# Second output projection of a two-block layer: second half of the outputs tile by tile, with the norm per tile

## The chip, the cores and the metric

One core of a Trainium2 chip runs the whole program. The metric is the device time of one execution in microseconds. Engines are named as the profile names them: PE (matmuls), PEld (weight loads of PE), DVE, ACT, POOL and SP; SP issues most transfers.

## What is computed

The program is two transformer blocks in a row on 512 tokens of width 1024. The change lies in the second block, between its mixer and its feed-forward part (names of the reference, shortened):

```python
merged = sigmoid(g_attn) * (attn @ w_attn_out) + sigmoid(g_hy) * (hy @ w_hy_out)
out = merged @ w_out                      # 512 x 1024 by 1024 x 1024
x = x + g1 * out
h = rmsnorm(x, norm_ffn_g) * (1 + sc2) + sh2
x = x + g2 * peer(h, wq, keys1, keys2, u_tab, v_tab)
```

`peer` looks up 16 of 16,384 experts per token and head. The kernel takes the rows of `u_tab` and `v_tab` for the last 128 tokens by gathers, and for the first 384 tokens multiplies by the whole tables.

## The kernel before

Tokens lie in four tiles of 128 (`NT` = 4, `ND` = 3 of them dense in `peer`). The tile framework takes the program as it is written, sets the order of each engine's instructions with its own timing model, and inserts the waits; each engine then runs its instructions in that order. A buffer of a pool (`bufs=n`) is taken over by the next tile of that name when the last reader of the old one is done.

Every fp32 product is made of three: `split` (L66 to L70) copies an operand to a rounded `hi` on ACT (L69) and subtracts it on DVE, or on POOL, to get `lo` (L70); `mm3` (L85 to L89) multiplies hi by hi, lo by hi and hi by lo. `wload` (L72) fetches a weight chunk of 512 KB into `wraw` (4 buffers) and splits it into `whi` and `wlo` (3 buffers each).

The stage in question is at the start of `peer`:

- `out_proj` (L431) multiplies `merged` (split as `mh`, `ml`) by `w2o`, which is 8 chunks: 4 for the first 512 outputs, 4 for the others. For each half it takes one PSUM bank (`bank`, 6 of them) per token tile, goes through the 4 chunks, and for each chunk through the tiles, 6 matmuls each (24 per tile and half). Then it adds the gated result to the residual `x` in two DVE operations (L452, L453).
- It is called twice, for tiles 0 to 2 and for tile 3 (`groups`, L1446), so the 8 chunks are fetched and split twice.
- Then the norm: `sumsq` (L859) squares a tile's row on ACT with a running sum (L863), `row_rstd` (L108 to L119) makes the inverse root in two DVE steps, one ACT root (L114) and four DVE steps, once for tiles 0 to 2 and once for tile 3. `modulated_tile` (L842) scales the row into `xn` (L847), transposes it on PE in 8 pieces of 128 x 128 (L853), evacuates each from PSUM with scale and shift into `hf` on DVE (L854), and splits that into `hph` and `hpl`, in two halves of 4 pieces.
- After the last tile is written down, `ahead(4)` (L1436) computes 4 of the 128 products of the dense part early: `u_chunk` (L1422) fetches and splits a chunk of `puT` (lo on POOL here), makes 24 matmuls on the first 384 tokens into `acc` (2 banks), applies gelu on ACT (L1430) and stores the result.
- `scores` (L1522) follows: the query projection (`pwq`) on all 512 tokens, the router's first product.

Of the kernel before, what the change touches and what calls it, by code (L numbers as in the profile page):

```python
# [9 lines left out]
F32 = mybir.dt.float32  # L10
F32R = mybir.dt.float32r
# [4 lines left out]
AF = mybir.ActivationFunctionType  # L16
ALU = mybir.AluOpType
# [4 lines left out]
D = 1024  # L22
KD = D // 128
NT = S // 128
# [22 lines left out]
class Emit:  # L47
# [383 lines left out]
    def out_proj(self, wd, mh, ml, tiles, gate=None, pool=None, fill=None):  # L431

        nc = self.nc
        for n in range(2):
# [11 lines left out]
            for p, t in zip(po, tiles):  # L446
# [3 lines left out]
                else:  # L450
                    tmp = pool.tile([128, 512], F32, name="gtmp", bufs=2)
                    nc.vector.tensor_tensor(tmp, p, gate[:, n * 512:(n + 1) * 512], op=ALU.mult)  # L452
                    nc.vector.tensor_tensor(xs, tmp, xs, op=ALU.add)  # L453


    def moe(self, fill):
        tc, nc, A = self.tc, self.nc, self.A
# [381 lines left out]
            self.split(hh[:, k, :128 * n], hl[:, k, :128 * n], f)  # L839
            yield xn  # L840

    def modulated_tile(self, t, rstd, a, b, hh, hl, pool):  # L842

        nc = self.nc
        xn = pool.tile([128, D], F32, name="xn", bufs=2)
        c = slice(t * 128, t * 128 + 128)
        nc.scalar.activation(xn, self.x[:, t], AF.Copy, scale=rstd)  # L847
        for kk in range(0, KD, 4):
            p = self.bank()
            f = pool.tile([128, 512], F32, name="hf", bufs=2)  # L850
            for k in range(4):
                o = slice(k * 128, k * 128 + 128)
                nc.tensor.transpose(p[:, o], xn[:, (kk + k) * 128:(kk + k) * 128 + 128], self.ident)  # L853
                nc.vector.tensor_scalar(f[:, o], p[:, o], a[:, kk + k:kk + k + 1], b[:, kk + k:kk + k + 1],  # L854
                                        op0=ALU.mult, op1=ALU.add)
            self.split(hh[:, kk:kk + 4, c], hl[:, kk:kk + 4, c], f.rearrange("p (k t) -> p k t", k=4))
        return xn

    def sumsq(self, pool, xs, n, name):  # L859
        ssq = self.small.tile([128, n], F32, name=name)  # L860
# [534 lines left out]
    def peer(self):  # L1395
        tc, nc, A = self.tc, self.nc, self.A
# [3 lines left out]
        ND = NT - 1  # L1400
# [4 lines left out]
        with ExitStack() as es:  # L1405
            pp = es.enter_context(tc.tile_pool(name="pp", bufs=1))
            hh = pp.tile([128, KD, S], F32R, name="hph")
            hl = pp.tile([128, KD, S], F32R, name="hpl")
# [11 lines left out]
            a = self.mod_cols(pp, self.mod, 4 * D, "pa", self.vec[:, V_GF2:V_GF2 + KD])  # L1420
            b = self.mod_cols(pp, self.mod, 3 * D, "pb")
            def u_chunk(c, eng=None):  # L1422

                wh, wl = self.wload(A["puT"][c], eng=eng)
                p = self.acc()
                for k in range(KD):
                    s_ = slice(k * 128, k * 128 + 128)
                    self.mm3(p[:, :TD], wh[:, s_], wl[:, s_], hh[:, k, :TD], hl[:, k, :TD], k == 0, k == KD - 1)
                g = dn.tile([128, TD], F32, name="ga", bufs=4)
                nc.scalar.activation(g, p[:, :TD], AF.Gelu_apprx_tanh)  # L1430
                if c < AHEAD:
                    self.dma(ad[c], g)
                    return None
                return g

            def ahead(n, eng=nc.gpsimd):  # L1436
                for _ in range(n):
                    if nu[0] < AHEAD:
                        u_chunk(nu[0], eng)
                        nu[0] += 1  # L1440

            nu = [0]
            with ExitStack() as e2s:
                pm = e2s.enter_context(tc.tile_pool(name="pm", bufs=1))
                mh, ml, g1, mg = self.merged
                groups = range(NT - 1), [NT - 1]  # L1446
                for tiles in groups:
                    self.out_proj(A["w2o"], mh, ml, tiles, gate=g1, pool=mg)
                for tiles in groups:
                    n = len(tiles)  # L1450
                    ssq = self.sumsq(pm, lambda j: self.x[:, tiles[j]], n, f"ssq{n}")
                    rstd = self.row_rstd(ssq, n, f"rr{n}")
                    for j, t in enumerate(tiles):
                        xn = self.modulated_tile(t, rstd[:, j:j + 1], a, b, hh, hl, pm)
                        if t == NT - 1:
                            ahead(4)
                r1 = pm.tile([128, D], F32, name="r1")
                r2 = pm.tile([128, D], F32, name="r2")
                self.dma(r1, self.mod[0:1, 4 * D:5 * D].to_broadcast([128, D]))
                self.dma(r2, A["g_ffn2"].to_broadcast([128, D]))  # L1460
                stt(r1, r1, 1.0, r2, op0=ALU.add, op1=ALU.mult)
                self.dma(r2, self.mod[0:1, 3 * D:4 * D].to_broadcast([128, D]))
                tt(ht, xn, r1, op=ALU.mult)
                tt(ht, ht, r2, op=ALU.add)

# [48 lines left out]
            with ExitStack() as ek:  # L1514
# [98 lines left out]
                for t in range(ND):  # L1613
                    c = slice(t * 32, t * 32 + 32)
                    p = self.bank()
# [13 lines left out]
            with ExitStack() as ek:  # L1629
# [8 lines left out]
                for t in range(ND):  # L1638
                    for q in range(32):

                        e = eT[:, t * 32 + q].rearrange("p j n i -> p (j n) i")
                        o = p2.tile([128, 8, 64, 2], F16, name="oh", bufs=3)
                        tt(o, ih[:, None].to_broadcast([128, 8, 64, 2]),
                           e[:, 0:8, None].to_broadcast([128, 8, 64, 2]), op=ALU.is_equal)
                        w = p2.tile([128, 8, 64, 2], F16, name="ohw", bufs=3)
# [3 lines left out]
                        p = self.bank()  # L1649
                        for i in range(4):  # L1650
                            for j in range(2):
# [3 lines left out]
                                             scale=1.0 / WSCALE)  # L1655
                        n = 32 * t + q + 1
# [290 lines left out]
```

## Time and profile before

| | us |
|---|---|
| median of 3 runs | 2715.93 |
| lowest and highest run | 2709.26 and 2721.87 |
| the profiled execution | 2710.84 |
| its span in the profile | 2709.1 |
| PE busy, share of the span | 2445.6 (90%) |
| DVE busy | 1824.4 (67%) |
| ACT busy | 1090.5 (40%) |
| POOL busy | 939.3 (35%) |

The span is the time from the first to the last instruction that the profile shows; the 1.7 us between it and the profiled execution lie around it. Busy shares are averages over stages with different limits. PEclk is the clock that was granted to PE: 1.00 is 2.4 GHz, 0.50 is 1.2 GHz. In a timeline the brackets hold an engine's idle time before an instruction and what ended it.

### The profile page before, as it was taken

The page shows a single profiled execution, that of the slowest core. Times are in us where ns is not written, and L with a number is a line of the kernel's source. Part 1 is how long each engine was busy: PE and PEld are TensorE (multiplying, and loading weights), DVE is VectorE, ACT ScalarE, POOL GpSimd, SP SyncE. Part 2 cuts the span into 40 slices and gives each one's busy share as a digit, 9 for nine tenths or more (in the row PEclk, how much of TensorE's full clock was granted, in tenths as well). Part 3 has the DMA queues.
Part 4 walks back from the last instruction along what each step waited for, and adds up shares of the span by engine and source line. Part 5 has one row for each costly group of instructions (what it writes and reads, how often), then busy time and mean ns, then how long its engine had stood idle before and what let it go on. Part 6 is the DMA issues. An engine that isn't in the chain of part 4 may idle for free.

```text
span 2709.1 us, 33479 instructions
## 1 busy us (share of the span) xinstructions
PE 2445.6 (90%) x11725; PEld 1911.1 (71%) x11725; DVE 1824.4 (67%) x3149; ACT 1090.5 (40%) x1688; POOL 939.3 (35%) x777
## 2 busy tenths in 40 slices
PE   7999897879977988989798889989899999999997
PEld 6776566423335766668587778979688878888886
DVE  6677965334346576564648889977877767767676
ACT  5555434212215336653444554434433333333233
POOL 1002640111100310000145665420676765666661
PEclk9999998889988988999899999989899999999998
DMA  4114684789975211104534448997699988888884
GB/s 143 63 56 170 226 291 159 283 336 391 400 274 212 94 59 47 39 31 144 186 114 136 148 159 305 348 347 276 197 299 301 305 299 266 291 300 284 275 294 152
DMA packets 215934, 589.47 MB, mean 218 GB/s; under 512 B 30565, under 2 KB 85349, under 8 KB 214740
## 3 DMA queue, kind: packets, MB, share of 16 engines
q1 hardware_dynamic: 170836, 433.91, 45.9%
q0 software_dynamic: 44928, 153.42, 16.1%
q8 instruction: 92, 1.51, 0.2%
q14 instruction: 78, 0.64, 0.1%
HBM read 541.85 MB, written 53.78 MB: 220 GB/s over the span
## 4 chain that ended last, share of the span: by engine, by line
PE 30%; DVE 12%; DMA 10%; issue 9%; ACT 4%; POOL 3%; POOLq 0%; SPq 0%; DVEq 0%; ACTq 0%
DMA wraw<-puT 5%; PE acc L87 4%; PE acc L89 4%; PE acc L88 4%; PE yp L87 4%; PE yp L88 4%; PE yp L89 4%; DMA grow<-pvr,ei 3%; POOL grow L1493 2%; DVE wlo L70 2%; DMA gd<-gs 1%; PE bank L87 1%; PE bank L89 1%; PE bank L88 1%; DVE gy L1510 1%
## 5 line engine op out<-in xcount | busy, mean ns | idle before, releaser
L69 ACT ACTIVATE whi<-wraw 128x1024 fp32r<-128x1024 f32 (+1 forms) x290 | 300.0, 1035 | 478.1 <-PE acc L88 164.2
L87 PE MATMUL acc<-hph,whi 128*128 128x384 f32 (+1 forms) x1152 | 404.3, 351 | 20.8 <-ACT ga L1430 19.9
L89 PE MATMUL acc<-hph,wlo 128*128 128x384 f32 (+1 forms) x1152 | 402.6, 350 | 6.5 <-DVE wlo L70 5.6
L88 PE MATMUL acc<-hpl,whi 128*128 128x384 f32 (+1 forms) x1152 | 399.4, 347 | 0.0
L70 DVE TENSOR_TENSOR wlo<-wraw,whi 128x1024 fp32r<-128x1024 f32 (+1 forms) x242 | 294.9, 1220 | 138.4 <-ACT whi L69 136.5
L70 POOL TENSOR_TENSOR wlo<-wraw,whi 128x1024 fp32r<-128x1024 f32 x48 | 115.7, 2416 | 481.4 <-ACT whi L69 468.2
L87 PE MATMUL yp<-vhi,wah 128*128 128x512 f32 x732 | 231.0, 395 | 17.4 <-ACT wah L69 17.4
L87 PEld LDWEIGHTS acc<-hph,whi 128*128 128x128 f32 x1152 | 220.5, 191 | 32.8 <-ACT ga L1430 24.6
L89 PEld LDWEIGHTS acc<-hph,wlo 128*128 128x128 f32 x1152 | 220.2, 191 | 19.5 <-DVE wlo L70 12.1
L88 PE MATMUL yp<-vlo,wah 128*128 128x512 f32 x732 | 231.1, 395 | 0.0
L89 PE MATMUL yp<-vhi,wal 128*128 128x512 f32 x732 | 228.3, 395 | 0.0
L88 PEld LDWEIGHTS acc<-hpl,whi 128*128 128x128 f32 x1152 | 220.5, 191 | 7.1 <-DVE hpl L70 0.2
L1685 POOL TENSOR_TENSOR gw<-gw,ga 128x256 f32<-128x256 f32 x128 | 175.8, 1374 | 137.9 <-DMA ga<-ad 76.7
L1493 POOL DMA_INDIRECT grow<-pu,ei x128 | 151.0, 1179 | 209.4 <-DVE grow L1506 173.3
L70 DVE TENSOR_TENSOR vlo<-wraw,vhi 128x1024 fp32r<-128x1024 f32 x122 | 157.6, 1292 | 93.5 <-ACT vhi L69 93.5
L1493 POOL DMA_INDIRECT grow<-pvr,ei x128 | 177.0, 1383 | 119.4 <-DVE gy L1510 96.3
L69 ACT ACTIVATE wah<-gw 128x384 fp32r<-128x384 f32 x126 | 66.2, 526 | 276.7 <-POOL gw L1686 223.3
L1510 DVE SCALAR_TENSOR_TENSOR gy<-grow,wt,gy 128x1024 f32<-128x1024 f32 x127 | 164.0, 1291 | 16.2 <-DMA grow<-pvr,ei 14.2
L87 PEld LDWEIGHTS yp<-vhi,wah 128*128 128x128 f32 x732 | 139.8, 191 | 47.8 <-ACT wah L69 20.4
L70 DVE TENSOR_TENSOR wal<-gw,wah 128x384 fp32r<-128x384 f32 x126 | 94.1, 747 | 104.2 <-ACT wah L69 103.7
L89 PEld LDWEIGHTS yp<-vhi,wal 128*128 128x128 f32 x732 | 139.6, 191 | 31.1 <-DVE wal L70 1.8
L88 PEld LDWEIGHTS yp<-vlo,wah 128*128 128x128 f32 x732 | 139.6, 191 | 27.7
(671 smaller groups left out, 5154.6 us busy)
## 6 DMA issues: line engine op xcount, KB each, us to landing
wraw<-wgu SPq DMA_DIRECT2D x128, 512.0 KB
wraw<-puT SPq DMA_DIRECT2D x128, 512.0 KB
wraw<-pv SPq DMA_DIRECT2D x128, 512.0 KB
wraw<-wd SPq DMA_DIRECT2D x64, 512.0 KB
aw<-wada SPq DMA_DIRECT2D x48, 512.0 KB
gd<-gs SPq DMA_DIRECT2D x8, 2048.0 KB
gw<-gd SPq DMA_DIRECT2D x128, 128.0 KB
ad<-ga SPq DMA_DIRECT2D x80, 192.0 KB
```

What stands on the lines that cost most here:

```text
L69: nc.scalar.activation(hi, src, AF.Copy)
L70: (eng or nc.vector).tensor_tensor(lo, src, f32(hi), op=ALU.subtract)
L87: mm(ps, lhsT=wh, rhs=xh, start=first, stop=False)
L88: mm(ps, lhsT=wh, rhs=xl, start=False, stop=False)
L89: mm(ps, lhsT=wl, rhs=xh, start=False, stop=last)
L1493: nc.gpsimd.indirect_dma_start(out=r, out_offset=None, in_=A["pu" if i < 128 else "pvr"], in_offset=bass.IndirectOffsetOnAxis(ap=ei[:, s:s ...
L1510: stt(gy, r, wt[:, s:s + 1], gy, op0=ALU.mult, op1=ALU.add)
L1685: nc.gpsimd.tensor_tensor(gw[:, :TG], gw[:, :TG], g[:, :TG], op=ALU.mult)
```

## The change

- A new generator `out_proj_tiles` makes the first half of the outputs for all four tiles (4 banks, 4 chunks). It then fetches the 4 chunks of the other half once and keeps them: two in buffers of their own (`wo..`), two in the usual `whi` and `wlo`. The gated adds of the first half follow, and then each tile gets its 24 matmuls of the second half, its gated add, and is yielded.
- For each tile that is yielded, the caller makes the sum of squares (written into `xn` instead of a buffer of its own), `row_rstd` for this tile alone, and `modulated_tile`. In it the pieces are evacuated in turn by DVE and by ACT.
- `ahead(4, None)` is called behind tile 2 instead of behind tile 3, and its `lo` parts are subtracted on DVE.
- The loads of `r1` and `r2`, which `htok` needs, are written ahead of the stage.

```diff
@@ -451,6 +451,47 @@
                     tmp = pool.tile([128, 512], F32, name="gtmp", bufs=2)
                     nc.vector.tensor_tensor(tmp, p, gate[:, n * 512:(n + 1) * 512], op=ALU.mult)
                     nc.vector.tensor_tensor(xs, tmp, xs, op=ALU.add)
+
+    def out_proj_tiles(self, wd, mh, ml, gate, pool, wpool):
+
+
+        nc = self.nc
+
+        def add(p, t, n):
+            o = slice(n * 512, n * 512 + 512)
+            tmp = pool.tile([128, 512], F32, name="gtmp", bufs=2)
+            nc.vector.tensor_tensor(tmp, p, gate[:, o], op=ALU.mult)
+            nc.vector.tensor_tensor(self.x[:, t, o], tmp, self.x[:, t, o], op=ALU.add)
+
+        def mms(p, t, c, w):
+            for kk in range(2):
+                k, o = 2 * c + kk, slice(kk * 512, kk * 512 + 512)
+                self.mm3(p, mh[:, k, t * 128:(t + 1) * 128], ml[:, k, t * 128:(t + 1) * 128],
+                         w[0][:, o], w[1][:, o], k == 0, k == KD - 1)
+
+        ps = [self.bank() for _ in range(NT)]
+        for c in range(4):
+            w = self.wload(wd[c])
+            for t in range(NT):
+                mms(ps[t], t, c, w)
+        ws = []
+        for c in range(4):
+            if c < 2:
+                r = self.wraw.tile([128, 1024], F32, name="wraw")
+                self.dma(r, wd[4 + c])
+                w = [wpool.tile([128, 1024], F32R, name=f"wo{i}{c}", bufs=1) for i in range(2)]
+                self.split(w[0], w[1], r)
+            else:
+                w = self.wload(wd[4 + c])
+            ws.append(w)
+        for t in range(NT):
+            add(ps[t], t, 0)
+        for t in range(NT):
+            p = self.bank()
+            for c in range(4):
+                mms(p, t, c, ws[c])
+            add(p, t, 1)
+            yield t
 
 
     def moe(self, fill):
@@ -839,10 +880,9 @@
             self.split(hh[:, k, :128 * n], hl[:, k, :128 * n], f)
             yield xn
 
-    def modulated_tile(self, t, rstd, a, b, hh, hl, pool):
+    def modulated_tile(self, t, rstd, a, b, hh, hl, pool, xn):
 
         nc = self.nc
-        xn = pool.tile([128, D], F32, name="xn", bufs=2)
         c = slice(t * 128, t * 128 + 128)
         nc.scalar.activation(xn, self.x[:, t], AF.Copy, scale=rstd)
         for kk in range(0, KD, 4):
@@ -851,10 +891,13 @@
             for k in range(4):
                 o = slice(k * 128, k * 128 + 128)
                 nc.tensor.transpose(p[:, o], xn[:, (kk + k) * 128:(kk + k) * 128 + 128], self.ident)
-                nc.vector.tensor_scalar(f[:, o], p[:, o], a[:, kk + k:kk + k + 1], b[:, kk + k:kk + k + 1],
-                                        op0=ALU.mult, op1=ALU.add)
+                if k % 2:
+                    nc.scalar.activation(f[:, o], p[:, o], AF.Identity, scale=a[:, kk + k:kk + k + 1],
+                                         bias=b[:, kk + k:kk + k + 1])
+                else:
+                    nc.vector.tensor_scalar(f[:, o], p[:, o], a[:, kk + k:kk + k + 1], b[:, kk + k:kk + k + 1],
+                                            op0=ALU.mult, op1=ALU.add)
             self.split(hh[:, kk:kk + 4, c], hl[:, kk:kk + 4, c], f.rearrange("p (k t) -> p k t", k=4))
-        return xn
 
     def sumsq(self, pool, xs, n, name):
         ssq = self.small.tile([128, n], F32, name=name)
@@ -1443,23 +1486,20 @@
             with ExitStack() as e2s:
                 pm = e2s.enter_context(tc.tile_pool(name="pm", bufs=1))
                 mh, ml, g1, mg = self.merged
-                groups = range(NT - 1), [NT - 1]
-                for tiles in groups:
-                    self.out_proj(A["w2o"], mh, ml, tiles, gate=g1, pool=mg)
-                for tiles in groups:
-                    n = len(tiles)
-                    ssq = self.sumsq(pm, lambda j: self.x[:, tiles[j]], n, f"ssq{n}")
-                    rstd = self.row_rstd(ssq, n, f"rr{n}")
-                    for j, t in enumerate(tiles):
-                        xn = self.modulated_tile(t, rstd[:, j:j + 1], a, b, hh, hl, pm)
-                        if t == NT - 1:
-                            ahead(4)
                 r1 = pm.tile([128, D], F32, name="r1")
                 r2 = pm.tile([128, D], F32, name="r2")
                 self.dma(r1, self.mod[0:1, 4 * D:5 * D].to_broadcast([128, D]))
                 self.dma(r2, A["g_ffn2"].to_broadcast([128, D]))
                 stt(r1, r1, 1.0, r2, op0=ALU.add, op1=ALU.mult)
                 self.dma(r2, self.mod[0:1, 3 * D:4 * D].to_broadcast([128, D]))
+                for t in self.out_proj_tiles(A["w2o"], mh, ml, g1, mg, pm):
+                    xn = pm.tile([128, D], F32, name="xn", bufs=2)
+                    ssq = self.small.tile([128, 1], F32, name="ssq1")
+                    nc.scalar.activation(xn, self.x[:, t], AF.Square, accum_out=ssq)
+                    rstd = self.row_rstd(ssq, 1, "rr1")
+                    self.modulated_tile(t, rstd, a, b, hh, hl, pm, xn)
+                    if t == ND - 1:
+                        ahead(4, None)
                 tt(ht, xn, r1, op=ALU.mult)
                 tt(ht, ht, r2, op=ALU.add)
```

What it moves on PE, at the end of the projection. Before, the last matmuls of the projection (`bank_9302` is tile 3's second half) stand ahead of all transposes (`xn_9371` is tile 0's, `xn_9397` tile 1's); further on the u products (`acc_9494`) follow tile 2's last transposes:

```order
L89 MATMUL bank_9302<-whi_9341,ml2_8546 128x512
L853 MATMUL bank_9373<-ident_73,xn_9371 128x128 [waits Activation_49]
L853 MATMUL bank_9385<-ident_73,xn_9371 128x128
L853 MATMUL bank_9373<-ident_73,xn_9371 128x128 [waits DVE_49]
L853 MATMUL bank_9399<-ident_73,xn_9397 128x128 [waits Activation_49]
...
L853 MATMUL bank_9437<-ident_73,xn_9423 128x128 [waits DVE_49]
L87 MATMUL acc_9494<-hph_9010,whi_9490 128x384 [waits Activation_49]
L87 MATMUL acc_9528<-hph_9010,whi_9524 128x384
L88 MATMUL acc_9494<-hpl_9011,whi_9490 128x384 [waits DVE_49]
```

With the change (`bank_9200` is the second half of tile 0, `bank_9266` of tile 1, `bank_9332` of tile 2; `xn_9228` is tile 0's row, `xn_9294` tile 1's):

```order
L89 MATMUL bank_9200<-whi_9184,ml2_8546 128x512
L893 MATMUL bank_9242<-ident_73,xn_9228 128x128 [waits Activation_49]
L893 MATMUL bank_9254<-ident_73,xn_9228 128x128 [waits DVE_49]
L87 MATMUL bank_9266<-wo00_9166,mh2_8545 128x512 [waits DVE_49]
L88 MATMUL bank_9266<-wo10_9167,mh2_8545 128x512
...
L893 MATMUL bank_9242<-ident_73,xn_9228 128x128 [waits Activation_49]
L893 MATMUL bank_9254<-ident_73,xn_9228 128x128 [waits Activation_49]
L893 MATMUL bank_9242<-ident_73,xn_9228 128x128 [waits DVE_49]
L893 MATMUL bank_9254<-ident_73,xn_9228 128x128 [waits DVE_49]
L893 MATMUL bank_9308<-ident_73,xn_9294 128x128 [waits Activation_49]
L893 MATMUL bank_9320<-ident_73,xn_9294 128x128
L87 MATMUL bank_9332<-wo00_9166,mh2_8545 128x512
```

The 24 matmuls of tile 0 are now followed by two transposes of tile 0, which wait for ACT, and then by the matmuls of tile 1; the other transposes of tile 0 stand among and behind these, and two of tile 1 ahead of tile 2's matmuls.

On DVE, from the add of tile 1 on (`gtmp_9291` is tile 1's; `hf_9243` and `hf_9255` hold tile 0's transposed halves; `rr1v_9297` begins tile 1's row factor), the rest of tile 0 and the norm of tile 1 now stand in each other's places:

```order
L898 TENSOR_SCALAR hf_9255<-bank_9254,pa_9026,pb_9029 128x128 [waits PE_49]
L463 TENSOR_TENSOR gtmp_9291<-bank_9266,g1_8547 128x512 [waits PE_49]
L898 TENSOR_SCALAR hf_9243<-bank_9242,pa_9026,pb_9029 128x128 [waits PE_49]
L898 TENSOR_SCALAR hf_9255<-bank_9254,pa_9026,pb_9029 128x128 [waits PE_49]
L464 TENSOR_TENSOR x_tok_8534<-gtmp_9291,x_tok_8534 128x512 [waits DVE_49]
L70 TENSOR_TENSOR hpl_9011<-hf_9243,hph_9010 128x4x128 [waits DVE_49,Activation_49]
L112 TENSOR_SCALAR rr1v_9297<-ssq1_9295 128x1 [waits Activation_49]
L113 RECIPROCAL rr1l_9299<-rr1v_9297 128x1 [waits DVE_49]
L70 TENSOR_TENSOR hpl_9011<-hf_9255,hph_9010 128x4x128 [waits Activation_49]
```

The evacuations of tile 0's third pieces come ahead of the add of tile 1, and a split of tile 0 ahead of and inside tile 1's row factor.

On PE ahead of the router (`acc_9596` and `acc_9506` are the fourth u product before and now, `acc_9665` and `acc_9635` the router's first). Before:

```order
L88 MATMUL acc_9596<-hpl_9011,whi_9592 128x384
L89 MATMUL acc_9596<-hph_9010,wlo_9593 128x384
L87 MATMUL acc_9665<-hph_9010,whi_9661 128x512 [waits Activation_49]
L88 MATMUL acc_9665<-hpl_9011,whi_9661 128x512 [waits DVE_49]
L89 MATMUL acc_9665<-hph_9010,wlo_9662 128x512 [waits Pool_49]
```

With the change:

```order
L89 MATMUL acc_9506<-hph_9010,wlo_9503 128x384
L893 MATMUL bank_9576<-ident_73,xn_9562 128x128 [waits Activation_49]
L893 MATMUL bank_9588<-ident_73,xn_9562 128x128 [waits Activation_49]
L893 MATMUL bank_9576<-ident_73,xn_9562 128x128 [waits DVE_49]
L893 MATMUL bank_9588<-ident_73,xn_9562 128x128 [waits DVE_49]
L87 MATMUL acc_9635<-hph_9010,whi_9631 128x512 [waits Activation_49]
```

The last transposes, tile 3's, have moved from inside the u products to right ahead of the router's first matmul.

## Rows read from the trace of the kernel before

**Rows 1.** Windows over the stage: busy us of each engine, then PEclk.

```profile
core 0: us, PE busy (x) PEld busy (x) DVE busy (x) ACT busy (x) POOL busy (x), PEclk, DMA share, GB/s
1283.99:1330.62 46.63, 46.10 (x192) 35.68 (x192) 27.82 (x34) 19.06 (x23) 0.70 (x1) 1.00 0.58 188
1330.62:1355.41 24.79, 9.72 (x27) 4.50 (x27) 18.98 (x43) 10.97 (x17) 7.14 (x4) 0.59 0.49 176
1355.41:1358.86 3.45, 3.45 (x11) 3.23 (x11) 1.91 (x4) 0.47 (x1) 0.00 (x0) 0.50 0.00 0
1358.86:1374.82 15.96, 15.96 (x93) 15.50 (x93) 3.57 (x8) 6.72 (x9) 3.93 (x4) 1.00 0.26 78
1380.00:1420.00 40.00, 40.00 (x216) 36.52 (x215) 22.64 (x141) 16.07 (x31) 18.52 (x12) 1.00 0.42 136
```

**Rows 2.** Timeline of PE: start, duration, instruction, [idle before it].

```profile
1324.25 0.50 PE L88 MATMUL bank<-wlo,mh 128*128 128x512 f32 x1 [0.33 <-DVE wlo L70]
...
1324.82 0.40 PE L87 MATMUL bank<-whi,mh 128*128 128x512 f32 x1
...
1325.52 0.40 PE L87 MATMUL bank<-whi,mh 128*128 128x512 f32 x1
...
1355.41 1.01 PE L87 MATMUL acc<-hph,whi 128*128 128x384 f32 x2 [0.85 <-ACT hph L69]
...
1363.15 0.33 PE L87 MATMUL acc<-hph,whi 128*128 128x384 f32 x1
...
1363.67 0.33 PE L87 MATMUL acc<-hph,whi 128*128 128x384 f32 x1
...
1374.82 0.39 PE L87 MATMUL acc<-hph,whi 128*128 128x512 f32 x1
```

**Rows 3.** Groups of the norm's operations: ns minimum/median/maximum.

```profile
L452 DVE TENSOR_TENSOR gtmp<-bank,g x8: 682/684/687, 1299.1 to 1334.8; 128x512 f32<-128x512 f32 x8
L453 DVE TENSOR_TENSOR x_tok<-gtmp,x_tok x8: 683/687/691, 1300.3 to 1335.5; 128x512 f32<-128x512 f32 x8
...
L863 ACT ACTIVATE sqj<-x_tok x4: 1041/1044/1051, 1318.9 to 1338.0; 128x1024 f32<-128x1024 f32 x4
L863 ACT ACTIVATION_READ_ACCUMULATOR sqj<-x_tok x4: 184/186/192, 1319.8 to 1338.9; 128x1 f32 x4
...
L847 ACT ACTIVATE xn<-x_tok,rr3y x3: 1139/1152/1154, 1335.0 to 1340.3; 128x1024 f32<-128x1024 f32 x3
```

**Rows 4.** Timelines of DVE and ACT: the kernel's last norm, and a table load.

```profile
2703.16 0.15 DVE L112 TENSOR_SCALAR rr1v<-ssq 128x1 f32<-128x1 f32 x1
...
2703.55 0.20 ACT L114 ACTIVATE rr1y<-rr1l 128x1 f32<-128x1 f32 x1 [1.44 <-DVE rr1l L113]
...
2704.36 0.16 DVE L118 TENSOR_TENSOR rr1y<-rr1y,rr1l 128x1 f32<-128x1 f32 x1
...
2674.48 1.28 ACT L114 ACT_TABLE_LOAD   x1
```

**Rows 5.** Groups that read or write the tile hf: evacuations and splits.

```profile
L854 DVE TENSOR_SCALAR hf<-bank,pa,pb x32: 402/410/413, 1336.7 to 1370.2; 128x128 f32<-128x128 f32 x32
...
L836 ACT ACTIVATE hf<-bank,m2b,m2a x4: 764/778/781, 831.1 to 840.4; 128x512 f32<-128x512 f32 x4
...
L69 ACT ACTIVATE hph<-hf x8: 612/616/633, 1341.4 to 1371.8; 128x512 fp32r<-128x512 f32 x8
L70 DVE TENSOR_TENSOR hpl<-hf,hph x8: 683/688/693, 1342.0 to 1372.5; 128x512 fp32r<-128x512 f32 x8
```

**Rows 6.** Windows over idle stretches of PE and a burst after one.

```profile
1335.00:1335.50 0.50, 0.00 (x0) 0.00 (x0) 0.50 (x1) 0.50 (x1) 0.00 (x0) 0.60 0.10 41
...
993.00:998.22 5.22, 0.00 (x0) 0.00 (x0) 3.80 (x7) 2.25 (x6) 0.00 (x0) 0.90 0.31 104
998.22:1004.00 5.78, 5.78 (x12) 3.88 (x13) 3.63 (x3) 0.44 (x1) 0.00 (x0) 0.50 0.44 136
1004.00:1005.00 1.00, 1.00 (x6) 0.82 (x5) 0.42 (x1) 0.54 (x1) 0.00 (x0) 0.99 0.00 0
```

**Rows 7.** Timeline of DVE: a small operation of the shared norm of three tiles.

```profile
1332.53 2.19 DVE L117 TENSOR_SCALAR rr3l<-rr3l 128x3 f32<-128x3 f32 x1
```

## The prediction

> **What bounds the kernel now.** I read the windows over the stage first. The second output projection begins at 1283.99 us and the first product of the router (the query projection of `scores`) at 1374.82: the stage is 90.8 us long. PE is busy for 46.1 of the first 46.6 us with 192 matmuls, then it idles: from 1330.62 to 1355.41, 24.8 us, it has 27 recorded small matmuls, the transposes [rows 1]. During that time DVE and ACT compute the norm of all tiles and evacuate the transposes. Then the four product groups of `ahead` follow (u products below, 24 matmuls each), the first 3.45 us of them at PEclk 0.50, and then the router at once [rows 1, 2]. Behind the stage PE is full (40.0 us of 40), so I take it that a microsecond won or lost here arrives at the end [rows 1].
>
> The PE timeline gives the prices at full clock. Three matmuls of 512 columns last 1325.52 − 1324.82 = 0.70 us, so 0.233 each; three u matmuls last 1363.67 − 1363.15 = 0.52, so 0.173 each [rows 2]. At PEclk 0.50, 11 u matmuls take 3.45 us, 0.314 each [rows 1]. Real work on PE is 192 × 0.233 = 44.8 and 96 × 0.173 = 16.6, together 61.4 us, and the change leaves it as it is. Some 29 of the 90.8 us are waits, transposes and low clock: that is what can be won.
>
> **The change, part by part.**
>
> *Half the weight loads and splits.* Eight transfers of 512 KB, eight ACT copies and eight DVE subtractions go. In the 46.6 us of the projection ACT is busy 19.1, DVE 27.8, and the DMA engines 0.58 of the time, while PE has no gap worth naming [rows 1]: they are hidden, and I count nothing. SP only issues earlier. The first half takes 96 × 0.233 = 22.4 us; its third and fourth weight chunks are needed after 11 and 17 us, and the splits of the kept weights that now stand ahead of the fourth (2 × 1.05 on ACT) fit well before that.
>
> *Tile by tile.* This decides. After the 24 matmuls of tile 0 the instruction order of PE has two transposes of tile 0, and only behind them tile 1's matmuls; tiles 1 and 2 are followed in the same way. These transposes read `xn`, which stands at the end of the whole norm of their tile, which begins with the tile's last matmul. So PE stands still three times for a whole norm. What the matmuls of the next tile do cover is the evacuation of the transposes, not the norm.
>
> The norm's length, from its rows: gated product 0.68, add 0.69, squares with the read of their sum 1.04 + 0.10 (the read overlaps), copy 1.15 [rows 3]; the chain of the row factor 2703.16 to 2704.52, 1.36 [rows 4]; and seven handoffs between engines, which I take at 0.05. That is **5.4 us** with nothing in between. On tile 0 a table load of 1.28 [rows 4] stands between squares and root. The first two small steps of the chain (0.4) run beside it: 5.4 + 0.9 = **6.2**. On tiles 1 and 2 the rest of the previous tile stands in the queues between: two DVE evacuations of 0.41 ahead of the add, two ACT evacuations and a copy `hph` of 0.62 ahead of the squares, another `hph` ahead of the root, `hpl` of 0.69 ahead of the chain's end [rows 5]. Following the three queues by hand I get **7.4** each. An ACT evacuation of 128 columns has no row: it lies between 0.20, the root on one column [rows 4], and 0.78 for 512 columns [rows 5]. I take 0.46, on the line between them; the bounds move each wait by 0.5.
>
> *Behind tile 3.* The u products need tile 2's last evacuations and splits; `ahead` now splits its weights on DVE instead of POOL, and the buffers of its second and third chunk come free only with tile 3's last matmuls. So a split's copy of 1.05, the evacuations, `hph` and `hpl` stand in a row: **4.8 us** of PE wait. Tile 3's norm runs beside 48 u matmuls (8.3 us) and is hidden. Its last two pairs of transposes now stand behind the last u product instead of inside one: pairs, evacuations, a gelu and `hph` make **3.8 us** ahead of the router, where there was no wait before [rows 2].
>
> *POOL.* It is busy for 7.1 us of today's idle stretch with splits of `ahead` [rows 1], and one small DVE step took 2.19 us there [rows 7] instead of 0.15 [rows 4]. Those splits are gone from POOL, so the sum has the small steps at their short times; if they are slow all the same, each wait grows by about 2, which the top of the range takes in for one.
>
> The sum at full clock: 61.4 + 6.2 + 7.4 + 7.4 + 4.8 + 3.8 + 2.2 (eight pairs of transposes among the matmuls; one of 128 columns has no row at full clock, lies below the 0.173 of a u matmul, and is taken at 0.14) = 93.2, against 90.8 now: **+2**. The waits are moved, not removed.
>
> *The clock.* PE ran out of work at 1330.6 and PEclk fell at about 1335.1; another idle stretch of 5.2 us also ended at 0.50 [rows 6]. The waits of 6.2, 7.4, 7.4 and perhaps 4.8 are of that size, so I expect each to end at the lower level, 1.2 GHz. Coming back cost 3.45 us at that level in this stage [rows 1], 5.8 at the other place [rows 6]; the lost share is 1 − 0.173/0.314 = 0.45, so 1.55 or 2.6 us each. Today's stage pays this once, and that is inside its 90.8. Four times 1.55 makes **+6**. The rule of the Trainium skill (TensorE: Matmul & The Clock Gate, section "Why this matters for your kernels") speaks against this change: it wants no idle gaps between bursts of matmuls, because they put the engine back to its slow level. By that rule the sum is +8, without it +2.
>
> So the stage grows by 2 + 6 = 8 us. On the scale of the profiled execution (2710.84, span 2709.1) that is 2719; the median of the three runs is 2715.93, 5 above, which gives 2724. I take **2721**.
>
> **The rivals.**
>
> *A: PE runs on.* If the next tile's matmuls went ahead of the waiting transposes, or the norm were much shorter, the three waits of 21 us and their three clock losses would go: 2 − 21 + 1.6 = −17, 2694 to 2699. For it: the matmuls of tiles 1 to 3 are independent work of 16.8 us, which is what the code's order suggests. Against it: at 1324.25 a matmul waits for its `wlo`, and the one at 1324.82, which needs only `whi`, stays behind it [rows 2]. The same page of the Trainium skill (section "Part 3: Packing small matmuls — row/col tiling") states that matmuls start and end strictly in program order and only weight loads are drawn ahead; by that rule A is out. 0.05.
>
> *B: the clock holds.* The transposes and the short bursts might keep PEclk up. Then +2: 2713 to 2718. Against it are the two falls [rows 6]. 0.15.
>
> *C: the clock stays low through all the bursts.* Each burst of 24 matmuls is followed by the next wait; if PE came back only in the u products, 72 matmuls would cost 0.233 × 0.314/0.173 = 0.42 instead of 0.233, 13.7 us, and the u products 1.55: 2 + 15 = +17, 2728 to 2733, slower. It decides if a burst, 19 matmuls in 8 us at the low level, ends before the clock rises. Against it: the clock rose after 3.45 and 5.8 us [rows 1, 6]. 0.10.
>
> **How the numbers follow.** The forecast (0.70) covers +4 to +13: two to four clock losses at 1.55 to 2.6, and the unknown evacuation. With B below and the lower part of C above, on both scales of the base time, 8 in 10 lie between 2706 and 2735. A change of 0.5%, 13.6 us, is about what a measurement here tells from none: under 2702.4 lies only A, 0.05; over 2729.5 most of C and the top of the forecast, 0.11; the rest, 0.84, is within.
>
> **What would show it.** Right: three idle stretches of PE of 6 to 8 us before pairs of transposes, each ended by `xn`; each next burst beginning at PEclk 0.50; the first router product 93 to 101 us behind the first projection matmul; a wait of some 4 us just ahead of it. Wrong: matmuls of tile 1 running before tile 0's transposes, norms of about 3 us, or a stage shorter than 85 us.

## The result, and the profile after

| | before | with the change |
|---|---|---|
| median | 2709.55 us (20 runs) | 2723.35 us (20 runs) |
| lowest and highest run | 2706.17 and 2721.87 | 2716.83 and 2732.95 |
| the profiled execution, its span | 2710.84, 2709.1 | 2724.25, 2722.5 |

The ratio is 1.0052, with a 95% interval from 1.0042 to 1.0062: the change costs 13.8 us (11.4 to 16.8 by the interval), at the edge of what was called a difference. The forecast was 2721, with "within 0.5%" as the likeliest case. The median of the kernel before, over more runs, lies 6 us under the 2715.93 that the forecast started from.

From the page of the changed kernel, its busy times and its memory traffic:

```profile
PE 2450.9 (90%) x11725; PEld 1918.6 (70%) x11725; DVE 1815.5 (67%) x3141; ACT 1086.7 (40%) x1698; POOL 926.7 (34%) x773
...
HBM read 537.65 MB, written 53.78 MB: 217 GB/s over the span
```

ACT has 3.8 us less work than before, DVE 8.9 and POOL 12.6, and eight loads of 512 KB are gone (541.85 MB were read before). None of it arrives at the end.

The windows over the stage, from the first `w2o` product (1292.21) to the first router product (1391.40) and on to the first product with `keys` (1407.27); the columns are those of [rows 1]:

```profile
1292.21:1320.47 28.26, 28.26 (x120) 22.46 (x120) 15.79 (x19) 6.94 (x8) 0.00 (x0) 1.00 0.61 201
1320.47:1326.68 6.21, 0.00 (x0) 0.00 (x0) 2.33 (x8) 3.78 (x5) 0.00 (x0) 0.70 0.03 13
1326.68:1334.19 7.51, 7.51 (x29) 6.02 (x30) 0.73 (x2) 0.80 (x2) 0.00 (x0) 0.79 0.01 2
1334.19:1341.36 7.17, 1.03 (x6) 0.42 (x4) 4.17 (x12) 4.13 (x8) 0.00 (x0) 0.91 0.00 0
1341.36:1349.93 8.57, 8.57 (x28) 6.83 (x29) 0.73 (x2) 0.81 (x2) 0.00 (x0) 0.68 0.00 0
1349.93:1357.10 7.17, 1.03 (x5) 0.41 (x3) 4.17 (x12) 4.13 (x8) 0.00 (x0) 0.76 0.00 0
1357.10:1364.90 7.80, 7.80 (x29) 6.12 (x29) 1.22 (x3) 1.58 (x3) 0.00 (x0) 0.78 0.00 0
1364.90:1368.35 3.45, 1.18 (x5) 0.43 (x5) 3.45 (x6) 2.49 (x6) 0.00 (x0) 0.85 0.44 144
1368.35:1391.40 23.05, 21.30 (x104) 19.98 (x104) 7.56 (x17) 11.84 (x20) 0.77 (x1) 0.87 0.48 171
1391.40:1407.27 15.87, 13.61 (x49) 11.27 (x49) 1.28 (x2) 2.01 (x3) 9.61 (x6) 0.68 0.37 119
```

After 28.3 us with PE full come three stretches in which PE stands or has only a pair of transposes, each followed by a burst that is partly at the lower clock. The stage is 99.2 us long (before: 90.8 [rows 1, 2]). The last window was 10.44 us long before:

```profile
1374.82:1385.26 10.44, 9.94 (x50) 8.62 (x50) 0.00 (x0) 2.99 (x4) 8.19 (x4) 1.00 0.56 185
```

The timeline of PE in the changed kernel, where it waited (start, duration, instruction, [idle before it and what ended it]); the counterparts of before are in [rows 2]:

```profile
1326.68 0.69 PE L893 MATMUL bank<-ident,xn 128*128 128x128 f32 x2 [6.21 <-ACT xn L887]
...
1335.45 0.65 PE L893 MATMUL bank<-ident,xn 128*128 128x128 f32 x2 [0.89 <-DVE hf L898]
...
1341.36 0.69 PE L893 MATMUL bank<-ident,xn 128*128 128x128 f32 x2 [5.26 <-ACT xn L887]
...
1357.10 0.69 PE L893 MATMUL bank<-ident,xn 128*128 128x128 f32 x2 [5.26 <-ACT xn L887]
...
1366.61 0.65 PE L893 MATMUL bank<-ident,xn 128*128 128x128 f32 x2 [1.15 <-DVE hf L898]
...
1368.35 1.01 PE L87 MATMUL acc<-hph,whi 128*128 128x384 f32 x2 [1.09 <-ACT hph L69]
...
1389.41 0.65 PE L893 MATMUL bank<-ident,xn 128*128 128x128 f32 x2 [0.40 <-DVE hf L898]
...
1391.40 1.12 PE L87 MATMUL acc<-hph,whi 128*128 128x512 f32 x2 [1.35 <-ACT hph L69]
...
1395.53 0.80 PE L89 MATMUL acc<-hph,wlo 128*128 128x512 f32 x1 [2.26 <-POOL wlo L70]
```

The three long waits end at `xn`, that is, with the norm. The last row is the new one: inside the router's first product PE waits 2.26 us for POOL. POOL's timeline there:

```profile
1392.81 0.24 POOL L1559 IOTA i<- 128x16 f16 x2 [22.72 <-DVE hpl L70]
1393.13 6.98 POOL L70 TENSOR_TENSOR wlo<-wraw,whi 128x1024 fp32r<-128x1024 f32 x3
```

POOL had been idle for 22.7 us. The IOTA (it fills `i16`, whose buffer follows on those of the stage) waits for the stage's last `hpl`, and the split of the router's weights is queued behind it. Before, the same IOTA started 1.5 us ahead of the router, and PE waited only 0.50 us for that split:

```profile
1373.29 0.25 POOL L1519 IOTA i<- 128x16 f16 x2 [6.52 <-DVE hpl L70]
```

Now it starts 1.4 us behind the router's first product.

So the stage is 8.4 us longer and the router's first part 5.4. Together, from the first projection product to the first `keys` product, it is 115.1 us against 101.3: 13.8 us, as much as the medians differ.

### The profile page after: what moved, and what is told of

The parts are those of the page before. It is cut to its first block, busy times and chain, and to the rows that moved or that the text cites. A ratio compares the mean times of both kernels' runs of the same rounds, so it can differ in the third digit from the quotient of the medians.

```text
span 2722.5 us, 33450 instructions
## 1 busy us (share of the span) xinstructions
PE 2450.9 (90%) x11725; PEld 1918.6 (70%) x11725; DVE 1815.5 (67%) x3141; ACT 1086.7 (40%) x1698; POOL 926.7 (34%) x773
## 5 line engine op out<-in xcount | busy, mean ns | idle before, releaser
L69 ACT ACTIVATE whi<-wraw 128x1024 fp32r<-128x1024 f32 (+1 forms) x280 | 289.1, 1033 | 479.6 <-PE acc L88 172.4
L70 DVE TENSOR_TENSOR wlo<-wraw,whi 128x1024 fp32r<-128x1024 f32 (+1 forms) x236 | 286.8, 1216 | 141.9 <-ACT whi L69 140.1
L1533 POOL DMA_INDIRECT grow<-pvr,ei x128 | 171.3, 1338 | 113.6 <-DVE gy L1550 88.3
L70 POOL TENSOR_TENSOR wlo<-wraw,whi 128x1024 fp32r<-128x1024 f32 x44 | 106.0, 2415 | 148.1 <-ACT whi L69 134.8
```

Source lines behind the costliest of these rows:

```text
L69: nc.scalar.activation(hi, src, AF.Copy)
L70: (eng or nc.vector).tensor_tensor(lo, src, f32(hi), op=ALU.subtract)
L1533: nc.gpsimd.indirect_dma_start(out=r, out_offset=None, in_=A["pu" if i < 128 else "pvr"], in_offset=bass.IndirectOffsetOnAxis(ap=ei[:, s:s ...
```

## The experiments

Beside the time, each run is read by two lengths: A, from the first `w2o` product to the first router product, and B, from there to the first `keys` product. The ratio is to the kernel before as it was timed beside that run, with its 95% interval; differences of medians between two edited kernels compare runs taken at different times.

| kernel | A | B | A + B | median | ratio |
|---|---|---|---|---|---|
| before | 90.8 | 10.4 | 101.3 | 2709.55 | |
| the change | 99.2 | 15.9 | 115.1 | 2723.35 | 1.0052 (1.0042 to 1.0062) |
| e2_iota | 99.3 | 12.6 | 111.9 | 2724.06 | 1.0046 (1.0028 to 1.0065) |
| e3_busy | 93.5 | 15.3 | 108.8 | 2717.95 | 1.0029 (1.0016 to 1.0042) |
| e4_pool | 100.2 | 15.3 | 115.5 | 2722.87 | 1.0048 (1.0032 to 1.0064) |
| e7_dve_evac | 99.7 | 15.7 | 115.3 | 2722.01 | 1.0042 (1.0025 to 1.0059) |
| e1_pipe | 83.7 | 14.9 | 98.6 | 2706.52 | 0.9985 (0.9972 to 0.9998) |
| e5_pipe_iota | 84.0 | 10.7 | 94.6 | 2708.06 | 0.9984 (0.9968 to 0.9999) |
| e9_tr | 87.1 | 11.8 | 98.9 | 2706.07 | 0.9991 (0.9979 to 1.0003) |
| e10_before_tr | 84.2 | 9.7 | 93.9 | 2705.53 | 0.9985 (0.9972 to 0.9997) |
| e8_pipe_tr | 73.3 | 9.7 | 83.0 | 2696.94 | 0.9950 (0.9936 to 0.9965) |
| e11_pipe_tr_dve | 73.4 | 9.7 | 83.1 | 2690.75 | 0.9939 (0.9919 to 0.9958) |

**The kernel before, again.** No edit.

> The kernel before, unchanged, for a second profile of it. In the one profile of each, the first product of the projection starts at 1284.0 us in the kernel before, and at 1289.1 to 1292.9 us in the five kernels that have the change, although nothing ahead of it was changed. If such a start belongs to the single execution, this profile may begin that stage anywhere from 1282 to 1294 us; if it belongs to the kernel, within 1 us of 1284.0. The last stretch, from the first second-layer product of the value weights on, took 771 us in the kernel before and 763 to 765 in three of the five: the same question, with 762 to 772 or 771.

This profile has the stage's start at 1288.6 us (first profile: 1284.0), A + B at 101.2 (101.3), and the last stretch at 758.3 (764.8), counted here from the first product with `vhi`; the 771 us of the expectation count from some 6 us earlier. The start and the last stretch therefore differ between executions of one kernel; over all thirteen profiles they range from 1284 to 1293 and from 753 to 766. The three profiles with the order of before have the three earliest starts, so it is not shown that chance is all of it; but most of the difference is there long before the stage: one product of the first block comes at 401.9 us in the first profile and at up to 409.9 in the others. A + B is what can be compared between single profiles: three kernels with the change's order gave 115.1, 115.3 and 115.5.

**POOL's queue ahead of the router.**

```diff
+            i16 = pp.tile([128, 2, 16], F16, name="i16")
+            for half in range(2):
+                nc.gpsimd.iota(i16[:, half], pattern=[[1 + 3 * half, 16]], base=0, channel_multiplier=0,
+                               allow_small_or_imprecise_dtypes=True)
...
-                i16 = pv.tile([128, 2, 16], F16, name="i16")
-                for half in range(2):
-                    nc.gpsimd.iota(i16[:, half], pattern=[[1 + 3 * half, 16]], base=0, channel_multiplier=0,
-                                   allow_small_or_imprecise_dtypes=True)
```

> The changed kernel with one thing moved: the two IOTAs that fill i16 on GpSimd are issued ahead of the projection, in a buffer of their own, and no longer stand in GpSimd's queue between the last hpl and the split of the first router weights. Theory 2 (this queue costs the 5.4 us between the first router product and the first keys product that the forecast left out, 15.9 us against 10.4 before): that split is done before the router begins, the wait of 2.3 us for wlo goes, and the 15.9 us become 10 to 13; the kernel 3 to 5.5 us faster than the changed kernel. Rival (the split is late for another reason, its buffer or its high half; or the 5.4 us is the low clock, and that stays): the wait may go, but the 15.9 us stay within 1.5 us, and the time within 2 us of the changed kernel.

POOL's timeline and the window from the first router product to the first `keys` product in this kernel:

```profile
1389.91 2.35 POOL L70 TENSOR_TENSOR wlo<-wraw,whi 128x1024 fp32r<-128x1024 f32 x1 [2.02 <-ACT whi L69]
```

```profile
1391.48:1404.09 12.61, 11.40 (x48) 10.04 (x48) 1.93 (x2) 2.06 (x4) 1.24 (x2) 0.87 0.22 67
```

The split starts ahead of the router, the wait for `wlo` is gone, and B falls by 3.3 us: that part of the theory holds. The other 2.2 us of the 5.4 stay, in a window at PEclk 0.87 where before it was 1.00. Two rows of this kernel say where: the first 3.2 us are at the lower clock, and ahead of the `keys` product there is a wait for ACT that neither kernel had:

```profile
1391.48:1394.70 3.22, 3.22 (x10) 3.12 (x11) 1.93 (x2) 0.47 (x1) 0.78 (x1) 0.50 0.47 140
```

```profile
1404.09 0.60 PE L1578 MATMUL bank<-keys,pq 128*128 128x128 f32 x3 [1.21 <-ACT pq L1574]
```

The time did not follow (2724.06, where 3 us less were expected); the interval, 1.0028 to 1.0065, is 10 us wide and does not tell 3 us from none.

**The clock in the waits.**

```diff
             add(p, t, 1)
+            if t < NT - 1:
+                d = self.acc()
+                for _ in range(5):
+                    nc.tensor.matmul(d, lhsT=self.ident, rhs=self.x[:, t, 512:1024], start=True, stop=True)
             yield t
```

> The changed kernel with extra work: behind the gate addition of tiles 0, 1 and 2, five float32 products of 128 x 512 that nobody reads, so that TensorE is busy in the later part of each of the three waits. Theory 3 (the waits also cost the clock: the bursts behind them start at half of the clock): the granted clock stays at 1.00 through the three bursts, they take 5.5 to 6 us each instead of 7.5 to 8.6, and the kernel is 4 to 6 us faster than the changed kernel, though it does more. Rival (the low clock in the records costs nothing, or the extra products hold up the transposes): the time within 2 us of the changed kernel, or slower.

Windows of this kernel (an extra product is two records there, so x10 is five): the first wait, filled; the burst of tile 1; the second wait and the burst of tile 2:

```profile
1317.96:1324.17 6.21, 4.56 (x10) 1.82 (x11) 2.33 (x8) 3.79 (x5) 0.00 (x0) 1.00 0.04 15
1324.17:1330.25 6.08, 6.08 (x28) 4.85 (x29) 0.73 (x2) 0.59 (x2) 0.00 (x0) 1.00 0.00 0
1330.25:1337.45 7.20, 5.80 (x16) 2.29 (x15) 4.17 (x12) 4.34 (x9) 0.00 (x0) 1.00 0.00 0
1337.45:1343.50 6.05, 6.05 (x28) 4.82 (x29) 0.73 (x2) 0.56 (x2) 0.00 (x0) 1.00 0.00 0
```

The waits are as long as they were, the clock stays at 1.00, and the bursts take 6.1 us instead of 7.5 and 8.6. A falls by 5.7 us and the median by 5.4, with more work on PE. The lower clock behind the waits has a price, and this is it.

**Two parts of the change undone.** First, the lo splits of `ahead` on POOL; second, all evacuations on DVE.

```diff
-                        ahead(4, None)
+                        ahead(4)
```

> The changed kernel with one part of the change undone: the low halves of the first four u weights are split on GpSimd again, as in the kernel before, no longer on VectorE. Theory A (VectorE's four splits of 1.2 us stand in its queue between the last tiles' evacuations, and where they stood there they were on the path): the stage to the first router product is 1 to 3 us shorter than 99.2, and so is the time. Theory B (these splits are covered on either engine): the stage within 1 us of 99.2, the time within 2 us of the changed kernel. Theory C: GpSimd, at 2.4 us a split, has its queue moved back, and the first router weights come later: the wait for wlo grows over 2.3 us and the kernel is slower by as much.

```diff
-                if k % 2:
+                if False:
```

> The changed kernel with another part of the change undone: all eight evacuations of a tile's transposes on VectorE, as before, none on ScalarE. What it tells is whether these evacuations stand on the path. Theory A (each wait of TensorE ends at xn, ahead of the evacuations, so that only those of the last tile are open): 0 to 2 us longer between the first u product and the router, nothing elsewhere; the time within 2 us of the changed kernel. Theory B (the transposes follow their evacuations in pairs, so every tile is held): four more of 0.4 us on VectorE for each of four tiles, 4 to 6 us slower.

A + B is 115.5 and 115.3 where the change has 115.1, and both times lie within 1.5 us of it. Theory B of the first holds. Of theory A of the second the total holds (A is 0.5 us longer), not the place: up to the first u product the stage is 2.0 us longer, and behind it 1.5 us shorter. Neither part matters in this order of the work.

**The next tile's products ahead of the norm.**

```diff
-        for t in range(NT):
+        def half(t):
             p = self.bank()
             for c in range(4):
                 mms(p, t, c, ws[c])
+            return p
+
+        nxt = half(0)
+        for t in range(NT):
+            p = nxt
+            if t + 1 < NT:
+                nxt = half(t + 1)
             add(p, t, 1)
             yield t
```

> The changed kernel, with one thing more: the 24 second-half products of tile t + 1 are issued ahead of tile t's norm, so that on TensorE they stand ahead of tile t's first transposes. No work is added or left out. Theory 1 (the norms lie open because TensorE's queue is in order): the three idle stretches of 6.2, 7.2 and 7.2 us shrink to 2 us or less each, and the bursts behind them no longer run at the low clock, which had cost half of their 3.0, 5.5 and 3.4 us. From the first product of the projection to the first router product: 99.2 us now, 76 to 84 us expected; the kernel 14 to 22 us faster than the changed kernel, so 0 to 9 us faster than the kernel before, since the router's first products still wait for GpSimd. Rival (VectorE and ScalarE, which do each tile's norm, evacuations and splits in order, are the bound, and the waits only move behind tile 3): 93 us or more in the stage, within 6 us of the changed kernel.

> Both edits together: the next tile's products ahead of the norm, and the IOTAs ahead of the projection. Theories 1 and 2 together: the gains add up, 17 to 27 us faster than the changed kernel, 4 to 14 us faster than the kernel before. Rival (both gains come from the same wait, since without the three waits the last hpl is early enough for GpSimd): no more than 2 us faster than the first edit alone.

The first edit gives 83.7 us in A, within what was expected, and 2706.52: 17 us faster than the changed kernel, 3 faster than the kernel before. Two windows of it, while the bursts of tiles 2 and 3 run and behind them:

```profile
1327.40:1340.50 13.10, 12.52 (x58) 9.90 (x58) 5.78 (x16) 5.11 (x8) 0.00 (x0) 1.00 0.00 0
1340.50:1354.71 14.21, 6.14 (x17) 2.83 (x17) 10.32 (x28) 11.06 (x24) 0.77 (x1) 0.61 0.62 222
```

The norms no longer stop PE, but a new stretch of 14 us has come up behind the last burst: DVE and ACT are busy for 5.8 and 5.1 us of the first window, and the transposes that would have given them work come only in the second. The order of PE in this kernel has 18 transposes together there, and of the 8.4 us of waits between them 6.5 end at evacuations (`hf`), the other 1.9 at a step of a row factor (`rr1v`).

The second edit adds the early IOTA. B falls by 4.2 us (3.3 in e2_iota) to 10.7, now at full clock, and the time again does not show it (2708.06, an interval 8 us wide):

```profile
1373.07:1383.74 10.67, 9.91 (x48) 8.61 (x48) 1.95 (x2) 2.06 (x4) 1.26 (x2) 1.00 0.27 82
```

Whether those 3 to 4 us arrive at the end was not settled by the times of these two pairs.

**Transposes first, evacuations after.** In the change as in the kernel before, the four transposes into one bank and their four evacuations are written in turn, and each transpose behind the first waits for the evacuation of the one ahead of it (in the order shown with the change: the third and fourth transposes into `bank_9242`, `waits Activation_49` and `waits DVE_49`).

```diff
             for k in range(4):
                 o = slice(k * 128, k * 128 + 128)
                 nc.tensor.transpose(p[:, o], xn[:, (kk + k) * 128:(kk + k) * 128 + 128], self.ident)
+            for k in range(4):
+                o = slice(k * 128, k * 128 + 128)
                 if k % 2:
```

This edit alone, on the changed kernel:

> The changed kernel with the four transposes of a bank ahead of its four evacuations, and the norm left where the change puts it, behind its tile's products. It tells which of the two edits of the last kernel carries the gain. Theory (each wait is a tile's norm, and only the place of the next tile's products decides): the three waits ahead of xn stay, 6 to 7.5 us each, and only the pairs of transposes at the stage's end get shorter; 94 to 98 us from the first product to the first router product, the kernel 2 to 6 us faster than the changed kernel and still slower than the kernel before. Rival (turn-taking of transposes and evacuations was what held TensorE in the changed kernel too): 85 us or less, faster than the kernel before.

The timeline of PE where it waits in this kernel, and its windows from tile 3's burst on:

```profile
1323.48 1.97 PE L893 MATMUL bank<-ident,xn 128*128 128x128 f32 x8 [6.21 <-ACT xn L887]
...
1336.93 1.97 PE L893 MATMUL bank<-ident,xn 128*128 128x128 f32 x8 [5.32 <-ACT xn L887]
...
1350.48 1.97 PE L893 MATMUL bank<-ident,xn 128*128 128x128 f32 x8 [5.32 <-ACT xn L887]
```

```profile
1350.48:1357.90 7.42, 7.42 (x30) 6.28 (x31) 2.93 (x6) 3.39 (x7) 0.00 (x0) 0.77 0.00 1
1357.90:1376.15 18.25, 18.25 (x108) 18.08 (x107) 10.87 (x19) 14.64 (x21) 0.77 (x1) 1.00 0.65 234
1376.15:1387.94 11.79, 10.19 (x49) 8.57 (x49) 0.00 (x0) 2.98 (x4) 9.70 (x6) 1.00 0.54 173
```

The three waits stay, as the theory said; but its number was far off (87.1, not 94 to 98, and 17 us faster than the changed kernel, not 2 to 6). The rival's 85 us are not met either. All eight transposes of a tile now go ahead of the next burst, so DVE and ACT evacuate and split tile 0 while tile 1's products run: 2.9 and 3.4 us in the last burst's window, where the changed kernel had 1.2 and 1.6. Window by window against the changed kernel, the second and third wait lose 1.0 each, the bursts 1.9 together, the 3.45 us behind tile 3 go, the u products with the wait ahead of the router lose 4.8 and stay at PEclk 1.00, and B loses 4.1: 16.2 us.

The control, the same edit on the kernel before:

> The kernel before with the same order of transposes and evacuations, and nothing else changed: the control for the best version. Theory (there the norm of three tiles together and the splits behind it are the wait, not the order of transposes): 88 to 91 us from the first product to the first router product where it was 90.8, the time within 3 us of the kernel before. Rival (the order of transposes alone is worth as much as in the best version): 80 us or less, 10 us faster than the kernel before.

```profile
1340.94 3.67 PE L853 MATMUL bank<-ident,xn 128*128 128x128 f32 x16 [5.56 <-ACT xn L847]
...
1345.01 1.92 PE L853 MATMUL bank<-ident,xn 128*128 128x128 f32 x8 [0.40 <-ACT xn L847]
...
1352.88 1.01 PE L87 MATMUL acc<-hph,whi 128*128 128x384 f32 x2 [5.95 <-ACT hph L69]
```

Neither theory is met: 84.2 us lies between 88 and 80. The transposes come in blocks of 16 and 8; what is left is a wait for `hph`. A + B falls by 7.4 us and the time by 4 (0.8 to 7.6).

Both edits on the changed kernel:

> The kernel with the next tile's products ahead of the norm, with one thing more: the four transposes of a bank are issued first, and the four evacuations after them. In the trace of the kernel with the first edit alone the transposes of tiles 0 to 2 are left in pairs, 18 of them behind tile 3's products, and TensorE waits for them from 1340 to 1354.7 us, at half of the clock. Theory (transposes and evacuations taken in turn hold the transposes back in TensorE's order): with eight transposes together behind each burst, that stretch of some 15 us becomes 5 or less; from the first product to the first router product 70 to 77 us instead of 83.7, the kernel 7 to 13 us faster than with the first edit alone. Rival (VectorE and ScalarE hold that stretch by their own work, 5 to 6 us in 7): 81 us or more, within 3 us of the first edit alone.

```profile
1326.98 1.09 PE L900 MATMUL bank<-ident,xn 128*128 128x128 f32 x8 [0.63 <-ACT xn L894]
...
1340.92 1.09 PE L900 MATMUL bank<-ident,xn 128*128 128x128 f32 x8 [0.79 <-ACT xn L894]
...
1345.99 1.01 PE L87 MATMUL acc<-hph,whi 128*128 128x384 f32 x2 [3.98 <-ACT hph L69]
```

A is 73.3 us, within the theory's range. Ahead of `xn` PE now waits 0.6 to 0.8 us, and the one long wait left, 4.0 us, is for tile 2's `hph`. The kernel is 0.50% faster than the kernel before (0.35 to 0.64%), 26 us faster than the changed kernel, and beats both. A + B is 18.3 us shorter than before, of which the time shows 13.6 (9.5 to 17.3).

> The best version so far (next tile's products ahead of the norm, transposes first) with all evacuations on VectorE, so that the part of the change that gives ScalarE half of them is undone. Theory (where the norms run beside the products, the two engines are what is left in the stage, and VectorE, busy for 5 us in 7, gets 1.6 us a tile more): 75 to 79 us instead of 73.3, 2 to 5 us slower than the best version. Rival (covered here too): within 1 us of 73.3.

The rival holds: A is 73.4 us, so ScalarE's half of the evacuations is covered here too. The median, 2690.75 from 4 runs, is not told apart from 2696.94 by the intervals.

## Why the prediction was right and wrong

**Hidden weight loads: right.** 120 products in 28.26 us are 0.2355 each, at PEclk 1.00 and without a gap. The work that was saved on ACT, DVE, POOL and the queues was never waited for.

**The norm on PE's path: right.** 6.2, 7.4 and 7.4 us were forecast; the stretches are 6.21, 7.17 and 7.17 long. The ACT evacuation, taken at 0.46 between 0.20 and 0.78, took 0.45 (median of 16), and the small DVE steps 0.15 to 0.16. PE kept its order, by which rival A was held out; the run that moves the next products ahead in that order takes the waits away.

**Around the u products: a little high.** 4.8 behind tile 3 were 3.45; 3.8 ahead of the router were 2.95 (from the end of the last u product at 1388.45).

**The clock: right in kind, low in size.** Four returns at 1.55 us were forecast. The windows of the changed kernel at the lower level are:

```profile
1326.68:1329.70 3.02, 3.02 (x8) 2.48 (x9) 0.73 (x2) 0.00 (x0) 0.00 (x0) 0.50 0.02 5
1341.36:1346.90 5.54, 5.54 (x14) 4.45 (x15) 0.73 (x2) 0.00 (x0) 0.00 (x0) 0.50 0.00 0
1357.10:1360.50 3.40, 3.40 (x9) 2.81 (x10) 0.73 (x2) 0.00 (x0) 0.00 (x0) 0.50 0.00 0
1368.35:1374.20 5.85, 5.85 (x17) 5.44 (x18) 4.05 (x11) 2.85 (x5) 0.77 (x1) 0.50 0.88 323
...
1391.10:1401.20 10.10, 7.54 (x17) 5.63 (x18) 1.29 (x2) 0.77 (x2) 7.22 (x5) 0.51 0.46 148
```

The first four are 17.8 us long; at the lost share of 0.45 that is 8.0 us instead of 6.2. e3_busy measures the price of the first three by itself, 5.7 us, where three times 1.55 is 4.7. The rule of the Trainium skill that was cited against the change (TensorE: Matmul & The Clock Gate, section "Why this matters for your kernels": no idle gaps between bursts) decides here as it says. Rival B is out, since every wait ended at 0.50; rival C too, since every burst got its clock back before it ended.

The waits were forecast 2.7 us too high in all and the clock 1.8 too low. These errors nearly cancel: 99.2 us were forecast for the stage (93.2 and 6), and it took 99.2. That the two agree to 0.1 us is luck.

**The step that failed** is "Behind the stage PE is full, so I take it that a microsecond won or lost here arrives at the end". It was full there in the kernel before; with the change it is not. The forecast's sum ends at the first router product; the 5.4 us behind it are missing. By the windows PE is idle there for 2.3 us instead of 0.5, and busy for 13.6 us instead of 9.9 with the same products: 1.8 us are a longer wait for POOL and 3.7 a lower clock.

The wait is POOL's queue: the IOTA waits for the last `hpl`, and the split of the router's weights behind it comes too late. The forecast had looked at POOL only as an engine that is relieved. Taking the IOTA out of the way (e2_iota) gives back 3.3 us, more than the wait, since the low clock then lasts 3.2 us from the first router product on, and not 9.8 (the last window above, from 1391.40 on). Of the 2.2 us left there 1.5 are a fifth loss of clock, and 0.7 the difference of two waits (1.21 for `pq`, 0.50 for `wlo` before). The wait ahead of the router was priced at 3.8 us, but no clock was counted for it. Where both causes are gone, in e5_pipe_iota, B is 10.7, near the 10.4 of before.

That 2723.35 lies 2.4 us from the forecast is therefore partly luck: the change was put at 5 to 8 us on a base of 2715.93, and it is 13.8 us on a base of 2709.55.

**What the forecast did not ask.** It took the pairs of transposes from the order as given. Their turns with the evacuations are worth 16.2 us in A + B (e9_tr), more than the whole change costs. With them gone the change as it stands is still behind (98.9 against 93.9 of e10_before_tr); with the next products ahead of the norm as well it is ahead (83.0). A is then 17.5 us under the kernel before, about the 17 that rival A gave for a PE that runs on; here the order was changed for it, and it took both edits.

The Trainium skill has a rule that asks for such a wait (PSUM — Partial Sum Buffer, section "PSUM bank collisions raise a hardware error": guard PSUM by its bank, not by the address). The trace agrees as far as it goes: the fourth transpose of a bank waited 0.9 us for the evacuation of the third, which lies in another part of that bank, and with the four transposes first no such wait is left. Whether the framework sets the wait because of the bank or because it takes the four parts as one tile, no run here shows.

## What to carry to other kernels

Work cut into pieces per tile hides a serial chain only if the next tile's products stand ahead of the chain's consumer in the in-order queue of the engine that is the bound; emit them one tile ahead, and read the queue's order to see it. Fill a PSUM bank with all its transposes before the first evacuation of it, or TensorE takes turns with the evacuating engines. End a forecast's sum not at the stage's last product but at the first one behind it that has no new wait, and count the clock for each idle stretch, also the last.

## What was not expected of the hardware

- The time from the start of a burst to the full clock differed: 3.0, 5.5, 3.4 and 5.9 us behind stretches of 3.5 to 7.2 us in which PE mostly stood, and 9.8 us where one more wait, of 2.26 us, lay inside. The forecast had two rows, 3.45 and 5.8 us, and priced all four returns by the shorter one, at 1.55 us; the 8.0 us of the four are 2.0 each, between its two prices.
- Two profiles of the unchanged kernel agree within 0.1 us on A + B, but differ by 4.6 us in when the stage starts and by 6.5 us in the last stretch of some 760 us. For differences of 3 us the stage's own length told more than the medians.
